# A hybrid decoder layer on one core: x and y loads queued behind weight loads, gamma and beta held in place, and the sum of probabilities on VectorE

## The chip, the core and the metric

The kernel runs on one core of a Trainium2 chip. The metric is device time in microseconds of one execution; the time before is the median of three runs. The engines are named as in the profile: PE is TensorE (PEld its weight loads), DVE is VectorE, ACT is ScalarE, POOL is GpSimd, and SP is SyncE, on whose queue every DMA of this kernel is issued. L122 is line 122 of the kernel before.

## The reference

One post-norm layer over a residual stream x of 1024 positions by 2048 channels, float32. Three mixers read the same x: attention with 8 heads of 128 and a forget gate, a short gated convolution, and causal pooling at four scales. Their gated outputs are concatenated, go through one output projection, and the result is normalised.

```python
proj = jnp.einsum('bsd,de->bse', x, w_in[l])
(q, k, v, g_att, fg, c_b, c_c, c_h, g_conv, p_u, g_pool) = jnp.split(proj, IN_SPLITS, axis=-1)
y_att  = forgetting_attention(q, k, v, fg, b_f[l]) * jax.nn.silu(g_att)     # heads apart
y_conv = short_conv_mixer(c_b, c_c, c_h, conv_w[l]) * jax.nn.silu(g_conv)
y_pool = multiscale_pool_mixer(p_u, pool_w[l], pool_scale[l]) * jax.nn.silu(g_pool)
y = jnp.concatenate([y_att, y_conv, y_pool], axis=-1)
y = jnp.einsum('bse,ed->bsd', y, w_out[l])
x = layer_norm(DEEPNORM_ALPHA * x + y, ln_g[l], ln_b[l])
```

Inside attention, per head: logits = q k / sqrt(128) + cum_q - cum_k, causal; p = softmax(logits); out = p v. The change touches the sum over the keys in this softmax, the loads of x for the last line, and the loads of ln_g and ln_b.

## The kernel before

**Numbers as pairs.** Every matmul operand is split into a high part, which ACT writes by a cast (L121), and a low part, which DVE writes by a subtraction (L122). A product is three matmuls (L128 high by high, L129 high by low, L130 low by high), all with 512 columns or fewer. So each weight tile `wh` of 128x512 costs one DMA load `wr` (256 KB), one ACT cast, one DVE subtraction, and feeds 12 matmuls. `t` is a tile of scores or probabilities, `pt` its split pair; `xy` and `xys` are split pairs of y or of sums of y blocks, loaded as `yr`.

**Stages.** The projection and the output product are each cut into 2x2 blocks and done with seven block products instead of eight. The first pass (0 to about 580 us) does four of the seven for 28 pairs of projection columns and keeps partial results in device memory. The second pass (to about 1256 us) does the other three for each pair; when a head's columns are ready, its attention runs beside the next pairs' matmuls, in small steps that `tick` takes from a list, one slot for every three matmul groups. Then come the output products, in the order y11, ys3, ys2, ys1, y22, y12, ys4, each twice (i = 0 and 1, the two halves of the columns), and the normalisation, whose steps for rows 512 and on run beside y12 and ys4, and for the first 512 rows beside and behind ys4.

**Attention of a head.** Scores are computed with the keys on the partitions, in blocks (n, j) of 128 keys j by up to 512 queries of half n: four blocks for n = 0, eight for n = 1. `find_top` takes the maximum over the keys through a small round trip by device memory (L746 writes `m_dram`, L748 loads it spread to all partitions as `mb`); `shift` (L759, DVE) subtracts it; `probs` (L765, ACT) takes the exponential; `parts` splits the block into `pt` (L121 on ACT, L122 on DVE); `values` multiplies by v on PE. `fold` (L712, and L710 for a first copy) adds a block to the running sum `m` over keys; before, it runs on POOL, just after the exponential. `invert` reduces that sum over the partitions (L735 to L745 on DVE) and makes the same round trip to `mb`, and `finish` multiplies by it (L798, DVE).

**What sets the order.** A scheduler with a simulated timeline places the instructions: each engine has one queue, worked off in order, and the scheduler may put an instruction ahead of others of the same queue if its simulated inputs and buffers are ready earlier. `keep_in_program_order` holds an instruction at its place; `issue_after` keeps the instructions of a block behind a given one on the same queue. Weight loads are made by `fill` (L184), in the order of `plan`; they take turns in four buffers `wr` with the `yr` and `wl` loads. `next_w` splits ahead: two weight tiles are held ready, from the ys2 product on four.

**Loads at the end.** `fetch` (L958) loads a y block, `load_x` (L1028) one of the 32 x tiles that are added to the result, into six buffers `st`, and `load_gb` (L1114) the four gamma and beta tiles of 512 KB, which are used first by the normalisation (L1144, L1145) beside y12.

Of the kernel before, what the change touches and what calls it, by code (L numbers as in the profile page):

```python
# [36 lines left out]
ALU = mybir.AluOpType  # L37
AX = mybir.AxisListType

P = 128  # L40
D = 2048
S = 1024
# [3 lines left out]
H = S // 2  # L46
# [27 lines left out]
def layer(ctx: ExitStack, tc: tile.TileContext, xt, x, wp, wf, b_f, conv_w, pool_w, pool_scale,  # L74
          w_out, ln_g, ln_b, out):
    nc = tc.nc
# [27 lines left out]
    def f4(name, tag):  # L104
        return tile_of([P, S], F32, name, tag)


    def hl(name, tag):
        return tile_of([P, 2, H], F32R, name, tag)

    def half(name, tag):
        return tile_of([P, H], F32, name, tag)
# [7 lines left out]
    def split(hi, lo, src):  # L120
        nc.scalar.copy(hi, src)  # L121
        nc.vector.tensor_tensor(lo, src, hi.bitcast(F32), ALU.subtract)  # L122

    def split_tile(t, src):
        split(t[:, 0], t[:, 1], src)
# [40 lines left out]
    def at(slot, step):  # L166

        while len(side) <= slot:
            side.append([])
        side[slot].append(step)  # L170
# [8 lines left out]
    stream = deque()  # L179
    ready = deque()  # L180
    plan = deque()
    ahead, n_split = [2], [0]

    def fill():  # L184
        while plan and len(stream) < 2:
            raw = half("wr", "wr")
            nc.sync.dma_start(raw, plan.popleft())
            stream.append(raw)

    def next_w():  # L190

        fill()
        while stream and len(ready) < ahead[0]:
            n_split[0] += 1
            t = hl("wh", "wx" if n_split[0] % 5 < ahead[0] - 2 else "wh")
            split_tile(t, stream.popleft())
            ready.append((t[:, 0], t[:, 1]))
            fill()
        return ready.popleft()
# [4 lines left out]
    def take(name, k, tag):  # L204
        xs[name, k] = hl("x" + name, tag)
        return xs[name, k]
# [460 lines left out]
    def attention(h, qs, ks, vt, gate):  # L667
        t, pt, v, o, top, down, total = {}, {}, {}, {}, {}, {}, {}
# [11 lines left out]
        def first(n, j):  # L680
            return max(0, j - 4 * n) * P
# [23 lines left out]
        def fold(kept, n, j, op, eng):  # L705
            c0 = first(n, j)
            if j == 1:
                kept[n] = half("m", "m")
                if c0:
                    eng.tensor_copy(kept[n][:, :c0], t[n, 0][:, :c0])  # L710
            prev = t[n, 0] if j == 1 else kept[n]
            eng.tensor_tensor(kept[n][:, c0:], prev[:, c0:], t[n, j][:, c0:], op)  # L712
# [49 lines left out]
        def probs(n, j):  # L762
            def go():
                tj, c0 = t[n, j], first(n, j)
                nc.scalar.activation(tj[:, c0:], tj[:, c0:], AF.Exp)  # L765
                if j:
                    fold(total, n, j, ALU.add, nc.gpsimd)
            return go

        def parts(n, j):  # L770
            def go():
                cw, th = min(first(n, j), 256), hl("pt", "pt")
                split(th[:, 0, cw:], th[:, 1, cw:], t[n, j][:, cw:])
                pt[n, j] = th
            return go

        def values(n, j):
# [26 lines left out]
        for n, s0, e0 in ((0, 3, 12), (1, 7, 20)):  # L804
            js = 4 * n + 4
            for j in range(js):
                at(s0 + j, scores(n, j))
                at(e0 + j, shift(n, j))
                at(e0 + j + 1, probs(n, j))
            for j in range(js):  # L810
                at(e0 + j + 2, parts(n, j))
                at(e0 + j + 3, values(n, j))
            at(s0 + js, find_top(n))
            at((4, 9)[n], turn_v(n))
            at(e0 + js + 2, invert(n))
            at(e0 + js + 7, finish(n))
# [141 lines left out]
    def fetch(name, k, slot):  # L958
        tag, src = BLOCKS[name]
        raw = []  # L960

        def load():
            raw.append(half("yr", "wr"))
            nc.sync.dma_start(raw[0], src(k))

        at(slot, load)
        at(slot + 2, lambda: split_tile(take(name, k, tag if isinstance(tag, str) else tag(k)), raw[0]))
# [60 lines left out]
    def load_x(name, i, st):  # L1028
        s, c = PLACE[name][0] + st, 2 * i + PLACE[name][1]
        xr = half("xr", "st")  # L1030
        nc.sync.dma_start(xr, x[s * P : s * P + P, c * H : c * H + H])
        return xr

    def residual_at(slot, i, st):

        env = {}

        def load():
            env["x"] = load_x("c22", i, st)

        def work():
            r = view("c22", i, st)
            nc.vector.scalar_tensor_tensor(r, env["x"], ALPHA, r, ALU.mult, ALU.add)
            stats_of(4 + st, r)

        at(slot, load)
        at(slot + 3, work)
# [4 lines left out]
    def preset_at(slot, name, i, st, tag):  # L1052


        env = {}

        def load():
            env["x"] = load_x(GOES_TO[name], i, st)

        def work():  # L1060
            acc = out_banks[name, i, st] = bank(tag)
            if name == "ys2":
                nc.scalar.copy(acc, view("c11", i, st))
            elif name == "ys4":
                nc.vector.scalar_tensor_tensor(acc, env["x"], ALPHA, view("c12", i, st), ALU.mult, ALU.add)
            else:
                nc.scalar.activation(acc, env["x"], AF.Copy, scale=ALPHA)

        if name != "ys2":
            at(slot, load)  # L1070
        at(slot + 3, work)
# [42 lines left out]
    def load_gb():  # L1114
        for src in (ln_g, ln_b):
            for hh in range(2):
                t = f4("gb", "gb")
                nc.sync.dma_start(t, src[hh * S : hh * S + S].partition_broadcast(P))
                gb.append(t)

    def norm_steps(s):
# [39 lines left out]
    def after(name, i):  # L1161
# [20 lines left out]
        if name == "y22":  # L1182
            for k in range(4 * i, 4 * i + 4):
                fetch("ys4", k, 1 + 2 * (k - 4 * i))
            if i == 0:
                at(9, load_gb)
            else:
                for st in range(4):
                    for n, step in enumerate(norm_steps(4 + st)):
                        at(1 + 5 * st + n, step)  # L1190
                for k in range(KH):
                    at(2 + 5 * k // 2, lambda k=k: load_last(1, k))
                    at(4 + 5 * k // 2, lambda k=k: split_last(1, k))
# [92 lines left out]
```

## Time and profile before

| | |
|---|---|
| time, median of 3 runs | 1631.89 us (1631.51 to 1632.08) |
| time of the profiled execution | 1629.22 us |
| its span, first to last instruction | 1627.5 us |
| mean granted clock of TensorE | 0.989 |
| POOL, folds of the sum (L712), 80 of them | 70.1 + 28.6 us |
| POOL, busy in all | 381.5 us |

The profiled execution lasts 1.7 us longer than its span, and 2.7 us less than the median of the runs. The rows of the views are read so: a group of instructions has line, engine, operation, tile written <- tiles read, shapes, count, then busy time, mean ns of one, and the engine's idle time before them with what ended it. A wait reads "engine tile line <- what ended it: us in total, times, longest". A window has its length, the busy time and count of PE, PEld, DVE, ACT and POOL, the granted clock, the mean busy share of the DMA engines, and GB/s. A timeline row has start, length (several instructions of one kind are merged), and in brackets the idle time before.

### The profile page before, as it was taken

Reading aid. Unit: us, or ns where it says so; the run is one execution under the profiler, and the core shown is the slowest. Engines: PE = TensorE matmul, PEld = TensorE weight load, DVE = VectorE, ACT = ScalarE, POOL = GpSimd, SP = SyncE. Lnnn points to the kernel's source line nnn. Section 1 sums busy time; section 2 is a strip of 40 time slices with the busy share of each in tenths; the row PEclk is TensorE's granted clock in tenths of the full one; section 3 lists DMA queues with packets and bytes.
Section 4 is the critical chain, followed back from the end, with each engine's and each line's share of the span. In section 5 each row is a group of like instructions: output and inputs, shape, how many; then the busy total and the mean of one; then the engine's idle time right before and its main releaser. Section 6 shows DMA issues by size and latency. Waiting matters only on the chain. (4 is left out here: it accounts for less than half of the span.)

```text
span 1627.5 us, 20130 instructions
## 1 busy us (share of the span) xinstructions
PE 1553.6 (95%) x6812; PEld 1254.3 (77%) x6812; DVE 1129.3 (69%) x1659; ACT 691.9 (43%) x1238; POOL 381.5 (23%) x303
## 2 busy tenths in 40 slices
PE   8999999999999999999999999999988998999986
PEld 6887888778787787788878777867766777788775
DVE  6754676666665656378787868577779875566797
ACT  4421221211121225566665656575666553444420
POOL 0232232222222220012232323343326322100000
PEclk9999999999999999999999999999999999999998
DMA  8756988887878667534545454535344445657572
GB/s 253 263 205 210 323 292 296 304 305 255 289 266 293 241 241 253 212 133 157 183 154 185 149 181 156 172 126 196 132 146 161 153 140 205 193 174 228 193 233 104
DMA packets 156807, 339.92 MB, mean 209 GB/s; under 512 B 17952, under 2 KB 27040, under 8 KB 156704
## 3 DMA queue, kind: packets, MB, share of 16 engines
q1 hardware_dynamic: 156704, 338.64, 61.2%
q8 instruction: 53, 0.87, 0.2%
q14 instruction: 50, 0.41, 0.1%
HBM read 247.28 MB, written 91.29 MB: 208 GB/s over the span
## 5 line engine op out<-in xcount | busy, mean ns | idle before, releaser
L122 DVE TENSOR_TENSOR wh<-wr,wh 128x512 fp32r<-128x512 f32 x264 | 199.4, 761 | 92.4 <-ACT wh L121 91.8
L121 ACT CAST wop<-wb 128x1024 fp32r<-128x1024 f32 x76 | 80.0, 1053 | 319.3 <-PE aux L129 139.2
L121 ACT CAST wh<-wr 128x512 fp32r<-128x512 f32 x264 | 161.5, 618 | 83.6 <-PE acc L130 27.9
L128 PE MATMUL acc<-x,wh 128*128 128x512 f32 x448 | 178.6, 399 | 3.3 <-ACT wh L121 3.3
L130 PE MATMUL acc<-x,wh 128*128 128x512 f32 x448 | 178.0, 397 | 3.4 <-DVE wh L122 3.4
L130 PE MATMUL aux<-xs,wop 128*128 128x512 f32 x448 | 175.5, 392 | 3.5 <-DVE wop L122 3.4
L129 PE MATMUL acc<-x,wh 128*128 128x512 f32 x448 | 176.3, 394 | 0.0
L128 PE MATMUL aux<-xs,wop 128*128 128x512 f32 x448 | 174.6, 390 | 0.0
L129 PE MATMUL aux<-xs,wop 128*128 128x512 f32 x448 | 174.4, 389 | 0.0
L122 DVE TENSOR_TENSOR wop<-wb,wop 128x1024 fp32r<-128x1024 f32 x76 | 102.7, 1352 | 27.1 <-ACT wop L121 27.0
L130 PEld LDWEIGHTS acc<-x,wh 128*128 128x128 f32 x448 | 84.7, 189 | 28.6 <-DVE wh L122 10.7
L130 PEld LDWEIGHTS aux<-xs,wop 128*128 128x128 f32 x448 | 84.1, 188 | 25.2 <-DVE wop L122 7.6
L128 PEld LDWEIGHTS acc<-x,wh 128*128 128x128 f32 x448 | 84.9, 190 | 22.5 <-ACT wh L121 7.2
L129 PEld LDWEIGHTS aux<-xs,wop 128*128 128x128 f32 x448 | 84.1, 188 | 17.7
L128 PEld LDWEIGHTS aux<-xs,wop 128*128 128x128 f32 x448 | 84.1, 188 | 17.5
L129 PEld LDWEIGHTS acc<-x,wh 128*128 128x128 f32 x448 | 85.0, 190 | 15.7
L130 PE MATMUL acc<-xs,wh 128*128 128x512 f32 x224 | 87.8, 392 | 3.4 <-DVE wh L122 3.4
L130 PE MATMUL acc<-xs,wop 128*128 128x512 f32 x224 | 88.0, 393 | 2.5 <-DVE wop L122 2.5
L122 DVE TENSOR_TENSOR pt<-t,pt 128x512 fp32r<-128x512 f32 (+1 forms) x96 | 84.5, 893 | 6.5 <-ACT pt L121 6.3
L128 PE MATMUL acc<-xs,wh 128*128 128x512 f32 x224 | 88.2, 394 | 0.0
L129 PE MATMUL acc<-xs,wh 128*128 128x512 f32 x224 | 87.4, 390 | 0.0
L128 PE MATMUL acc<-xs,wop 128*128 128x512 f32 x224 | 87.3, 390 | 0.0
(272 smaller groups left out, 3607.3 us busy)
## 6 DMA issues: line engine op xcount, KB each, us to landing
wb<-wp SPq DMA_DIRECT2D x116, 512.0 KB, 5.8
wr<-wp SPq DMA_DIRECT2D x112, 256.0 KB, 2.9
wo<-w_out SPq DMA_DIRECT2D x64, 256.0 KB, 6.0
o_dram<-wo SPq DMA_DIRECT2D x64, 256.0 KB, 4.5
wr<-o_dram SPq DMA_DIRECT2D x64, 256.0 KB, 2.8
t_dram<-wb SPq DMA_DIRECT2D x28, 512.0 KB, 5.8
a_dram<-ca SPq DMA_DIRECT2D x28, 512.0 KB, 3.8
b_dram<-cb SPq DMA_DIRECT2D x28, 512.0 KB, 4.6
```

Source lines behind the costliest of these rows:

```text
L121: nc.scalar.copy(hi, src)
L122: nc.vector.tensor_tensor(lo, src, hi.bitcast(F32), ALU.subtract)
L128: nc.tensor.matmul(acc, wh, xh, start=start, stop=False, **more)
L129: nc.tensor.matmul(acc, wh, xl, start=False, stop=False, **more)
L130: nc.tensor.matmul(acc, wl, xh, start=False, stop=stop, **more)
```

## The change

Three edits. `fill` remembers the last weight load that it traced, and the x loads and y loads are kept behind that one on the SP queue. The gamma and beta loads keep their place in the program. The fold of the sum moves from the step of the exponential to the step of the split, and from POOL to DVE.

```diff
     def fill():
         while plan and len(stream) < 2:
             raw = half("wr", "wr")
-            nc.sync.dma_start(raw, plan.popleft())
+            last_load[0] = nc.sync.dma_start(raw, plan.popleft()).ins
             stream.append(raw)
...
         def probs(n, j):
             def go():
                 tj, c0 = t[n, j], first(n, j)
                 nc.scalar.activation(tj[:, c0:], tj[:, c0:], AF.Exp)
-                if j:
-                    fold(total, n, j, ALU.add, nc.gpsimd)
             return go
 
         def parts(n, j):
             def go():
                 cw, th = min(first(n, j), 256), hl("pt", "pt")
                 split(th[:, 0, cw:], th[:, 1, cw:], t[n, j][:, cw:])
                 pt[n, j] = th
+                if j:
+                    fold(total, n, j, ALU.add, nc.vector)
             return go
...
         def load():
             raw.append(half("yr", "wr"))
-            nc.sync.dma_start(raw[0], src(k))
+            with tc.issue_after(last_load[0]):
+                nc.sync.dma_start(raw[0], src(k))
...
         xr = half("xr", "st")
-        nc.sync.dma_start(xr, x[s * P : s * P + P, c * H : c * H + H])
+        with tc.issue_after(last_load[0]):
+            nc.sync.dma_start(xr, x[s * P : s * P + P, c * H : c * H + H])
...
                 t = f4("gb", "gb")
-                nc.sync.dma_start(t, src[hh * S : hh * S + S].partition_broadcast(P))
+                tc.keep_in_program_order(nc.sync.dma_start(t, src[hh * S : hh * S + S].partition_broadcast(P)))
```

On VectorE, in the attention of a head (query half 1, blocks 0 to 3: `t` the probabilities, `pt` their split, `m` the sum, `wh` a weight split, L798 the end of the half before), the new order against the old:

```order
-L759 TENSOR_TENSOR t_5395<-t_5395,mb_5578 128x512
-L122 TENSOR_TENSOR pt_5728<-t_5353,pt_5728 128x512
-L122 TENSOR_TENSOR pt_5759<-t_5377,pt_5759 128x512
-L122 TENSOR_TENSOR wh_5738<-wr_5690,wh_5738 128x512
+L759 TENSOR_TENSOR t_5395<-t_5395,mb_5577 128x512
+L122 TENSOR_TENSOR pt_5726<-t_5353,pt_5726 128x512
+L712 TENSOR_TENSOR m_5759<-t_5353,t_5377 128x512
+L122 TENSOR_TENSOR pt_5756<-t_5377,pt_5756 128x512
+L712 TENSOR_TENSOR m_5759<-m_5759,t_5395 128x512
+L122 TENSOR_TENSOR wh_5736<-wr_5690,wh_5736 128x512
 L798 TENSOR_TENSOR pb_4809<-pb_4809,mb_5659 128x512
```

Two folds stand among the two splits; the fold of a block (here 5395) can stand ahead of that block's own split, since it needs the exponential alone.

On SP, at the end of ys3 and the start of ys2, before (`wr` weights from `o_dram`, `yr` sums of y, `xr` x tiles, `gb` gamma and beta):

```order
L964 DMA yr_11478<-sy_dram 128x512
L1031 DMA xr_12176<-x 128x512
L1031 DMA xr_12180<-x 128x512
L1031 DMA xr_12196<-x 128x512
L187 DMA wr_11486<-o_dram 128x512
L964 DMA yr_11500<-sy_dram 128x512
L1031 DMA xr_12198<-x 128x512
L1031 DMA xr_12217<-x 128x512
L1118 DMA gb_12711<-ln_g 128x1024
L187 DMA wr_11511<-o_dram 128x512
L1118 DMA gb_12713<-ln_g 128x1024
L964 DMA yr_11531<-sy_dram 128x512
```

With the change the weight and y loads stand there alone, and gamma and beta come about 105 DMAs later in the queue, among the first weight loads of y12 (`w_out`):

```order
L965 DMA yr_12670<-sy_dram 128x512
L187 DMA wr_12677<-w_out 128x512
L187 DMA wr_12696<-w_out 128x512
L1120 DMA gb_12711<-ln_g 128x1024
L1120 DMA gb_12713<-ln_g 128x1024
L1120 DMA gb_12715<-ln_b 128x1024
L1120 DMA gb_12717<-ln_b 128x1024
L187 DMA wr_12732<-w_out 128x512
L965 DMA yr_12746<-sy_dram 128x512
L187 DMA wr_12759<-w_out 128x512
L1033 DMA xr_12775<-x 128x512
```

The first x tile now stands where ys1 ends, and the others one to three at a time between weight loads.

On VectorE, at the end of the program (`bst` row statistics of the last product's two halves, 13300 and 13311; c_1909 and the three others the rows whose normalisation ends there), before:

```order
L1024 BN_STATS bst_12968<-acc_13300 128x6
L1133 TENSOR_SCALAR nt_13424<-mv_13420,nt_13424 128x1
L1024 BN_STATS bst_12968<-acc_13311 128x6
L1134 TENSOR_SCALAR nt_13424<-nt_13424,mv_13420 128x1
L1127 BN_AGGR mv_13490<-bst_12968 128x2
L1145 SCALAR_TENSOR_TENSOR c_1909_10844<-c_1909_10844,nt_13424,gb_12715 128x512
L1145 SCALAR_TENSOR_TENSOR c_2085_11772<-c_2085_11772,nt_13424,gb_12715 128x512
L1145 SCALAR_TENSOR_TENSOR c_1964_11125<-c_1964_11125,nt_13424,gb_12717 128x512
L1145 SCALAR_TENSOR_TENSOR c_2117_11953<-c_2117_11953,nt_13424,gb_12717 128x512
```

and with the change (L1147 is L1145 of before):

```order
L1025 BN_STATS bst_12968<-acc_13300 128x6
L1135 TENSOR_SCALAR nt_13424<-mv_13420,nt_13424 128x1
L1136 TENSOR_SCALAR nt_13424<-nt_13424,mv_13420 128x1
L1147 SCALAR_TENSOR_TENSOR c_1909_10844<-c_1909_10844,nt_13424,gb_12715 128x512
L1147 SCALAR_TENSOR_TENSOR c_2085_11772<-c_2085_11772,nt_13424,gb_12715 128x512
L1147 SCALAR_TENSOR_TENSOR c_1964_11125<-c_1964_11125,nt_13424,gb_12717 128x512
L1147 SCALAR_TENSOR_TENSOR c_2117_11953<-c_2117_11953,nt_13424,gb_12717 128x512
L1025 BN_STATS bst_12968<-acc_13311 128x6
L1129 BN_AGGR mv_13490<-bst_12968 128x2
```

Four L1145 moved from behind the last BN_STATS to ahead of it. On PE the change also puts the last two products in plain order: 96 matmuls of y12's second half, then 96 and 96 of ys4, where before 32 matmuls of ys4 stood among the last 20 of y12.

More of the change, by code (lines that the diff above doesn't have):

```diff
@@ L181, in layer @@
     plan = deque()
-    ahead, n_split = [2], [0]
+    ahead, n_split, last_load = [2], [0], [None]
     def fill():
```

## The prediction

> **What bounds the kernel now.** I read the page's busy times first, then the windows of the stretches that the change touches, then TensorE's waits in them, and last the timeline and the chain of waits at the places with the longest ones.
>
> ```profile
> span 1627.5 us, 20130 instructions
> PE 1553.6 (95%) x6812; PEld 1254.3 (77%) x6812; DVE 1129.3 (69%) x1659; ACT 691.9 (43%) x1238; POOL 381.5 (23%) x303
> ...
> 700.00:800.00 100.00, 100.00 (x466) 83.41 (x465) 77.30 (x130) 62.97 (x127) 23.64 (x24) 1.00 0.49 162
> ...
> 1200.00:1300.00 100.00, 88.05 (x389) 70.49 (x388) 85.48 (x140) 60.31 (x124) 39.00 (x34) 0.97 0.47 152
> 1300.00:1400.00 100.00, 89.47 (x382) 71.74 (x381) 61.08 (x100) 49.77 (x105) 19.88 (x20) 0.97 0.56 185
> 1400.00:1500.00 100.00, 100.00 (x443) 82.81 (x442) 62.49 (x97) 38.73 (x69) 6.26 (x4) 1.00 0.59 189
> ```
>
> TensorE (PE) is the bound: it is busy for 1553.6 of 1627.5 us, so everything that any change can win lies in the 73.9 us in which it is idle, and in the clock. Those idle times sit late. From 700 to 800 us, in the first heads of attention, there are none, from 1200 to 1400 us there are 22.5 us, and from 1400 to 1500 none again. (Columns: busy time of PE, PEld, DVE, ACT, POOL, then granted clock, DMA share, GB/s.) What ends them, from 560 to 1356 us (second pass and attention) and then to the end:
>
> ```profile
> PE aux L129 <- DVE pt L122: 12.7, 10, 2.5
> PE acc L128 <- ACT wh L121: 6.6, 4, 3.3
> ...
> PE acc L129 <- DVE wh L122: 4.9, 2, 4.1
> PE aux L128 <- ACT wh L121: 3.4, 2, 2.4
> PE acc L128 <- ACT wh L121: 1.7, 1, 1.7
> ```
>
> The largest is the low part of the split probabilities, `pt`, on VectorE (DVE): 12.7 us in ten waits. The last two rows are one place, 1378 to 1390 us (3.4 + 1.7 = 5.1 us in three waits). A long wait also costs clock:
>
> ```profile
> 1386.00:1394.00 8.00, 5.60 (x19) 4.16 (x18) 3.47 (x7) 5.95 (x12) 0.00 (x0) 0.79 0.70 226
> 1068.00:1078.00 10.00, 6.95 (x25) 5.07 (x24) 9.93 (x15) 4.36 (x11) 10.00 (x9) 0.85 0.23 71
> 1552.00:1562.00 10.00, 5.89 (x20) 4.65 (x20) 10.00 (x20) 2.36 (x4) 0.00 (x0) 0.83 0.76 247
> ```
>
> Behind the waits of 2.4, 2.5 and 4.1 us the granted clock is 0.79 over 8 us, 0.85 over 10 and 0.83 over 10: 8 x 0.21, 10 x 0.15 and 10 x 0.17 each give 1.5 to 1.7 us of lost clock. I price a dip at 1.6 us.
>
> [...]
>
> **Part 1: the sum of probabilities on VectorE.** Now GpSimd (POOL) folds, and VectorE splits and shifts beside it. One place out of eight alike, in the timeline, POOL first, then DVE, then PE:
>
> ```profile
> 912.88 1.63 POOL L871 TENSOR_TENSOR s3y<-pa 128x512 f32<-128x512 f32 x1
> 914.48 1.72 POOL L712 TENSOR_TENSOR m<-t,t 128x512 f32<-128x512 f32 x1
> 916.27 1.62 POOL L712 TENSOR_TENSOR m<-m,t 128x512 f32<-128x512 f32 x1
> ...
> 913.28 1.78 DVE L759 TENSOR_TENSOR t<-t,mb 128x512 f32<-128x512 f32 x1
> 914.99 3.45 DVE L122 TENSOR_TENSOR pt<-t,pt 128x512 fp32r<-128x512 f32 x2
> ...
> 916.80 0.50 PE L129 MATMUL aux<-pt,v 128*128 128x512 f32 x1 [1.29 <-DVE pt L122]
> ```
>
> The two splits take 1.72 us each, and end with the two folds, to a few hundredths; PE waits 1.29 us for the first. Free of POOL the same shape takes 0.68:
>
> ```profile
> L122 DVE TENSOR_TENSOR wlast<-wl,wlast 128x512 fp32r<-128x512 f32 x16 | 10.7, 682 | 1.1 <-ACT wlast L121 1.1
> ...
> 1066.46 0.42 DVE L759 TENSOR_TENSOR t<-t,mb 128x256 f32<-128x256 f32 x1
> 1066.80 0.28 DVE L723 TENSOR_TENSOR m<-m,t 128x128 f32<-128x128 f32 x1
> 1068.00 0.55 DVE L759 TENSOR_TENSOR t<-t,mb 128x384 f32<-128x384 f32 x1
> ...
> L122 DVE TENSOR_TENSOR pt<-t,pt 128x512 fp32r<-128x512 f32 x48 | 52.1, 1098 | 6.1 <-ACT pt L121 6.1
> L759 DVE TENSOR_TENSOR t<-t,mb 128x512 f32<-128x512 f32 x48 | 46.5, 982 | 15.1 <-DMA mb<-m_dram 15.1
> L122 DVE TENSOR_TENSOR pt<-t,pt 128x256 fp32r<-128x256 f32 x32 | 18.3, 573 | 0.3 <-ACT pt L121 0.3
> L122 DVE TENSOR_TENSOR pt<-t,pt 128x384 fp32r<-128x384 f32 x16 | 14.7, 918 | 0.1
> ...
> L712 POOL TENSOR_TENSOR m<-m,t 128x256 f32<-128x256 f32 (+1 forms) x64 | 70.1, 1095 | 59.8 <-ACT t L765 57.7
> L712 POOL TENSOR_TENSOR m<-t,t 128x384 f32<-128x384 f32 (+1 forms) x16 | 28.6, 1786 | 39.4 <-ACT t L765 34.5 <-DVE pa L908 4.9
> ```
>
> Removed from POOL: 80 folds (70.1 + 28.6 us) and eight small copies. Added to DVE, per head: query half 0 needs a copy of 128 columns and folds of 384, 256 and 128; half 1 four folds of 512 and one each of 384, 256, 128. That is 0.21 (estimate, below the 0.28 of two inputs) + 1.25 + 4 x 0.68 + 1.25 = 5.4 us, 43 us over eight heads. Given back: `pt` takes 48 x 1.098 + 32 x 0.573 + 16 x 0.918 = 85.7 us and would take 48 x 0.682 + 32 x 0.42 + 16 x 0.55 = 55.0 free of POOL, 31 too much; the 48 full shifts 48 x (0.982 - 0.682) = 14 too much. The ends for the relief are nothing (if the other POOL work takes the folds' place) and 31 + 14 = 45, and somewhat more with `wh` and the narrow shifts. POOL's folds start with the same exponential that releases the split, so I take it near the upper end: 40 us, an estimate. **VectorE's load then stays about as it is** (+3 us), but the part on PE's path, the split, comes first or nearly so.
>
> What PE wins: at the place above the shift (1.78) is held up by L871, which stays, and the split goes from 1.75 to 0.68, so of 1.29 us some 1.1 goes. Three heads look like this. I give the change two thirds of the 12.7 us, 8.4, and take 2.4 off, because in about half of the places the order puts a fold of 0.6 us ahead of the next split or weight split (the rows in the section on the change). One dip goes with the 2.5 us wait. Term: **-6.0 - 1.6 = -7.6 us**. Its bounds are +8 (the second rival) and -12.7 - 3.2. Behind a fold on DVE wait the weight splits `wh`; PE holds two of them ready, so 0.6 us is covered except where a `mb` transfer has just emptied the queue. POOL's remaining work stands off the path; the invert, which waited for POOL at L735, now waits for a fold just before it, and I cost that at nothing.
>
> **Part 2: x and gamma, beta leave the place at 1370 us.** The chain of waits there, then ACT's timeline, then the landing times of `gb`:
>
> ```profile
> 1371.63 6.60 DMA xr<-x
> 1378.30 6.58 DMA yr<-sy_dram
> ...
> 1389.84 2.71 DMA wr<-o_dram
> ...
> 1379.02 0.62 ACT L121 CAST wh<-wr 128x512 fp32r<-128x512 f32 x1 [2.15 <-DMA wr<-o_dram]
> 1383.06 0.62 ACT L121 CAST wh<-wr 128x512 fp32r<-128x512 f32 x1 [2.85 <-DMA wr<-o_dram]
> 1388.46 2.28 ACT L121 CAST wh<-wr 128x512 fp32r<-128x512 f32 x4
> ...
> DMA to landing us min/median/max: 6.0/7.0/7.9
> ```
>
> Six x tiles (256 KB each) and four gamma and beta tiles (512 KB each), 3.6 MB, are issued among the weight and y loads, long before anybody wants them. A load takes 6.6 us there instead of 2.7, ACT stands idle for it, and PE waits three times. In the new order of SP none of the ten is left there. The loads' own chain (2.7 + cast + split) stays, so I take 4.0 of the 5.1 us and the dip: **-4.0 - 1.6 = -5.6 us**; bounds 0 and -6.7.
>
> The ten transfers are not gone. The x tiles now come one or two at a time between weight loads; bursts of x tiles between 1400 and 1500 us cost PE nothing before either (its row above is 100 of 100). Gamma and beta move to just behind the fifth weight load of y12, some 145 us later, and the sixth load, a y load and the next weight load queue behind their 2 MB for 6 to 8 us. PE has four split weights ready there, about 11 us. I cost it at 0, with 4 us (6.6 - 2.7) as the upper end, plus a dip.
>
> **Part 3: the end.** The last normalisations fill VectorE (10.00 of 10 us in the window from 1552, above), and PE has its longest wait (4.1 us) for a weight split behind them.
>
> ```profile
> 1614.30 0.70 DVE L1024 BATCH_NORM_STATS2 bst<-acc 128x6 f32<-128x512 f32 x1 [0.22 <-PE acc L130]
> ...
> 1615.22 2.67 DVE L1145 SCALAR_TENSOR_TENSOR c<-c,nt,gb 128x512 f32<-128x512 f32 x4
> ...
> 1621.12 2.74 DVE L1145 SCALAR_TENSOR_TENSOR c<-c,nt,gb 128x512 f32<-128x512 f32 x4
> ```
>
> After the last matmul VectorE now does two groups of four L1145, 2.67 and 2.74 us. In the changed order the first group stands ahead of the last BN_STATS, beside PE's last 24 matmuls: **-2.6 us**. The long wait itself stays: between the eleventh and the twelfth weight split of y12 the old order has 14 other full-width instructions on VectorE and the new one 16, at 0.67 us each (2.67 / 4) 9.4 and 10.7 us. I cost that at 0, bounds -4 and +4.
>
> Sum: -7.6 - 5.6 - 2.6 = -15.8. I round to -15, as removed waits seldom vanish whole. The profiled execution took 1629.22 us, 2.67 below the median of the runs (1631.89); 1629.2 - 15 = 1614.2, and in the runs' terms **1616.9 us**.
>
> **The rivals.** (a) The waits pass on: PE is freed from `pt`, then waits for `wh` or `mb` a little later, and only a third of part 1 (-2.5) and the end (-2.6) are left with half of part 2 (-2.8): 1624. For it: waits for ACT's `wh` are 6.6 us of PE's idle time before 1356 us, and part 1 doesn't touch them. (b) Gamma and beta hit y12: the loads behind them are 4 us late, VectorE's unbroken stretch starts later, and 4 + 1.6 us come back: 1622.5. (c) **Slower:** the folds are blocked where POOL still works. POOL is busy for 39 of the 100 us from 1200; the folds are 98.7 / 8 = 12 us a head, so some 25 us of means, differences and sums of y stay there. If the 40 us of relief are cut by half, VectorE carries 20 us more, most of it in the four heads after 1000 us that already have waits; with 16 us of it on PE's path and parts 2 and 3 kept (-8.2) that is 1640. It decides once the folds' mean passes about 0.8 us. Against it: from 700 to 800 us DVE is idle for 23 of 100 us, and nothing of POOL but some 10 us stays. (d) The change not doing what it says is out: the rows of the orders show all three moves.
>
> [...]
>
> **How the numbers follow.** Forecast 0.55, (a) 0.2, (b) 0.13, (c) 0.08, and 0.04 for a larger gain. The range, 1608 to 1632: below, part 1 at -10 with two dips (-3.2), part 2 whole (-6.7) and the end (-2.6) make -22.5 and 1609; above, it takes in (a) and (b) and what both together would leave (1630), and it leaves (c) out. A measurement of this kernel can tell about 0.2%, 3.3 us, from no change: faster is below 1628.6, slower above 1635.2. Faster 0.8, same 0.11, slower 0.09.
>
> **What would show it.** Right: `pt` 128x512 near 0.75 us on average, DVE's busy time within 10 us of 1129; PE's wait for `pt` below 5 us; no wait over 1 us from 1370 to 1392; one L1145 group behind the last matmul. Wrong: L712 on DVE over 0.8 us; PE's waits for `wh` up by what those for `pt` fall; a new wait near 1520 to 1535 us behind `gb`; the long wait at 1552 us grown.

## The result and the profile after

| | before | after |
|---|---|---|
| time, median of four runs each | 1631.99 us (1631.51 to 1632.19) | 1622.75 us (1622.35 to 1624.12) |
| ratio, 95% interval | | 0.994 (0.9926 to 0.9953) |
| time of the profiled execution, its span | 1629.22, 1627.5 us | 1624.12, 1622.3 us |

The change is 9.2 us faster; the forecast was 15, its range held the time. Measured again (x1 below), the ratio was 0.991 (0.9887 to 0.9932), 14.7 us. The page of the change, then PE's waits from 560 to 1356 us, VectorE's groups in attention, and windows (columns as before):

```profile
span 1622.3 us, 20045 instructions
PE 1548.7 (95%) x6812; PEld 1253.5 (77%) x6812; DVE 1127.6 (70%) x1747; ACT 690.8 (43%) x1238; POOL 285.0 (18%) x215
```
```profile
PE acc L128 <- ACT wh L121: 7.9, 9, 1.2
PE acc L130 <- DVE wh L122: 7.2, 8, 2.8
PE aux L128 <- ACT pt L121: 6.7, 4, 2.3
PE aux L128 <- DVE m L725: 5.1, 3, 3.3
PE aux L129 <- DVE pt L122: 3.5, 7, 1.9
...
PE acc L129 <- DVE wh L122: 1.6, 1, 1.6
```
```profile
L122 DVE TENSOR_TENSOR pt<-t,pt 128x512 fp32r<-128x512 f32 x48 | 33.4, 698 | 1.7 <-ACT pt L121 1.7
L712 DVE TENSOR_TENSOR m<-m,t 128x512 f32<-128x512 f32 x24 | 16.3, 681 | 0.0
```
```profile
1200.00:1300.00 100.00, 89.33 (x388) 71.39 (x387) 86.86 (x158) 62.04 (x128) 27.88 (x24) 0.95 0.49 156
1300.00:1400.00 100.00, 96.80 (x432) 78.74 (x431) 62.91 (x118) 52.80 (x111) 9.46 (x9) 1.00 0.52 164
1400.00:1500.00 100.00, 98.77 (x436) 81.48 (x435) 65.24 (x102) 38.52 (x69) 6.27 (x4) 1.00 0.59 187
```

VectorE's load stayed (1129.3 to 1127.6), the split of a full block went from 1098 to 698 ns, and PE's wait for `pt` from 12.7 to 3.5 us. But its wait for ScalarE's half of `pt` grew to 6.7 us, from this row of before:

```profile
PE aux L128 <- ACT pt L121: 2.1, 2, 1.8
```

From 1200 to 1300 us hardly anything was won and the clock is lower (0.95, before 0.97); from 1300 to 1400 PE has 96.8 busy us instead of 89.5; from 1400 on there is a wait that was not there. Then the end, VectorE's timeline, with one group of L1147 (L1145 before) behind the last statistics, as forecast:

```profile
1607.98 2.74 DVE L1147 SCALAR_TENSOR_TENSOR c<-c,nt,gb 128x512 f32<-128x512 f32 x4
1611.39 0.70 DVE L1025 BATCH_NORM_STATS2 bst<-acc 128x6 f32<-128x512 f32 x1 [0.68 <-PE acc L130]
...
1615.88 2.74 DVE L1147 SCALAR_TENSOR_TENSOR c<-c,nt,gb 128x512 f32<-128x512 f32 x4
```

**Where the time went.** I counted PE's matmuls with weight tiles in order and compared the start of the same one in two traces. The table gives, for each run, by how many us a stretch is longer (+) or shorter than in the first profile of before (stretches in its time); the last column is the span's difference. The experiments' rows stand here too, since all are read from this table. Below, "the tail" is the stretch from 1476 us to the last matmul, and "the end" is what lies behind it.

| run | 0 to 703 | 703 to 1350 | 1350 to 1412 | 1412 to 1476 | 1476 to last matmul | behind it | span |
|---|---|---|---|---|---|---|---|
| before again (x9) | +3.4 | -1.3 | -0.2 | 0.0 | +2.5 | 0.0 | +4.4 |
| the change | +8.4 | -6.8 | -9.6 | 0.0 | +5.1 | -2.3 | -5.2 |
| the change again (x1) | +2.8 | -4.0 | -9.6 | 0.0 | +6.6 | -2.3 | -6.5 |
| sum alone (x2) | -0.8 | -4.2 | -6.4 | 0.0 | +3.1 | 0.0 | -8.3 |
| loads alone (x3) | +1.7 | -1.3 | -7.9 | 0.0 | +4.8 | -2.3 | -5.1 |
| gamma, beta free (x4) | +2.3 | -5.1 | -5.3 | 0.0 | +1.5 | 0.0 | -6.5 |
| sum on POOL, behind the split (x5) | +2.1 | -3.2 | -7.2 | 0.0 | +5.5 | -2.3 | -5.1 |
| sum on DVE, ahead of the split (x6) | +1.0 | -1.8 | -9.6 | 0.0 | +5.8 | -2.3 | -6.9 |
| x free (x7) | +0.1 | -5.8 | -8.6 | +0.7 | +5.9 | -2.3 | -10.0 |
| gamma, beta in ys1 (x8) | +3.7 | -3.0 | -10.3 | +3.9 | +1.8 | 0.0 | -4.0 |
| copies held (x10) | +4.7 | -22.6 | -7.2 | +0.3 | +6.1 | -2.3 | -21.1 |
| normalisation held (x11) | +1.1 | -9.5 | -10.5 | 0.0 | +1.6 | +2.1 | -15.1 |
| copies held, sum on POOL (x12) | +6.5 | -13.0 | -8.5 | +1.3 | +6.6 | -2.3 | -9.5 |

### The profile page after: what moved, and what is told of

It reads as the page before. It is cut to its first block, busy times and chain, and to the rows that moved or that the text cites. A ratio compares the mean times of both kernels' runs of the same rounds, so it can differ in the third digit from the quotient of the medians.

```text
span 1622.3 us, 20045 instructions
## 1 busy us (share of the span) xinstructions
PE 1548.7 (95%) x6812; PEld 1253.5 (77%) x6812; DVE 1127.6 (70%) x1747; ACT 690.8 (43%) x1238; POOL 285.0 (18%) x215
## 5 line engine op out<-in xcount | busy, mean ns | idle before, releaser
L128 PEld LDWEIGHTS acc<-x,wh 128*128 128x128 f32 x448 | 85.0, 190 | 26.5 <-ACT wh L121 10.9
L130 PE MATMUL acc<-xs,wop 128*128 128x512 f32 x224 | 87.9, 393 | 2.6 <-DVE wop L122 2.6
L128 PE MATMUL acc<-xs,wop 128*128 128x512 f32 x224 | 87.2, 389 | 0.0
L129 PE MATMUL acc<-xs,wop 128*128 128x512 f32 x224 | 87.2, 389 | 0.0
```

The costliest lines, as they stand in the source:

```text
L128: nc.tensor.matmul(acc, wh, xh, start=start, stop=False, **more)
L129: nc.tensor.matmul(acc, wh, xl, start=False, stop=False, **more)
L130: nc.tensor.matmul(acc, wl, xh, start=False, stop=stop, **more)
```

## The experiments

Each ratio is against runs of before on the same chip, made together with those of the run. Single executions of one program differ by several us (25 of before in the batch of x5 to x8: 1623.32 to 1641.42 us). The stretches differ less, but the seven profiles that have the same sum and the same copies (the change, x1, x2, x4, x7, x8, x11) still lie between -3.0 and -9.5 from 703 to 1350 us, so a difference of 2 or 3 us between two single profiles shows nothing in that stretch.

**x1, the change again.**

> The changed kernel once more, for its size and for how far two executions of one program lie apart. If the first pass (the same program in both kernels) differs only by chance, its end lies some microseconds away from that of the first profile of the change (which was 7.5 us later than in the profile of before), and the stretches behind it keep their differences. If the change itself slows the first pass, the five waits of 1.4 to 1.9 us in it come again at the same places. Time: 0.994 of before.

Ratio 0.991 (0.9887 to 0.9932). The first pass, the same instructions in both kernels, ends 6.4 us late in the first profile of the change and 2.3 late here; in the other runs it ends between 0.6 early and 5.6 late, and in before itself, run again, 3.6 late (x9). The first column is chance, then, and it hid most of what the first profile had won: without it the change wins 13.6 and 9.3 us in its two profiles.

**x2 and x3, one part at a time.** x2 has the fold's move alone, x3 everything but that.

```diff
 x2:  in parts:  +    fold(total, n, j, ALU.add, nc.vector)      loads as before
 x3:  in probs:  +    fold(total, n, j, ALU.add, nc.gpsimd)      loads as in the change
```

> The sum of probabilities on VectorE, loads as before. Theory (the three parts add up): -6 to -7.6 us, 1625, with the waits of 1378 to 1390 us and the long wait at 1552 us as before. Rival (the waits pass on to ScalarE's and VectorE's weight splits): -2.5 us or less, 1629.5. In both: pt 128x512 near 0.70 us.

> Loads of x, y, gamma and beta as in the change, the sum of probabilities on GpSimd as before. Theory (parts add up): the burst's place gives -9.7 us, the end -2.3, and the tail gives back 3 to 5 for a hole between the weight splits of y12: about -7 to -9, 1624. Rival (the burst's place gains so much only because the waits ahead of it had gone with the sum): -5 at that place, -2 to -4 in all, 1629.

Ratios 0.9937 (0.9915 to 0.9959) and 0.994 (0.9918 to 0.9961), about 10 us each, against 14.7 for both in the same batch: the parts seem not to add up, though the intervals of the three are wide (some 3.5 us each way). From 703 to 1350 us the sum gives its few us and the loads nothing that can be told from before run again (-1.3 both). The place from 1350 to 1412 us is where they overlap: both edits shorten it, the sum alone by 6.4, the loads alone by 7.9, together 9.6. Here are PE's waits in it, of before, of the sum alone, and of the loads alone:

```profile
PE aux L128 <- ACT wh L121: 3.4, 2, 2.4
PE acc L128 <- ACT c L1077: 1.9, 1, 1.9
PE acc L128 <- ACT wh L121: 1.7, 1, 1.7
```
```profile
PE aux L128 <- ACT wh L121: 3.3, 2, 2.4
PE acc L128 <- ACT wh L121: 0.6, 1, 0.6
```
```profile
PE aux L128 <- ACT wh L121: 1.3, 1, 1.3
PE acc L128 <- ACT c L1079: 0.5, 1, 0.5
```

The middle row of before is a wait at 1355 us for ScalarE to evacuate a bank, which the prediction had not counted. ScalarE's timeline of before there, with PE's matmul that waits:

```profile
1355.95 0.62 ACT L121 CAST xys<-yr 128x512 fp32r<-128x512 f32 x1 [1.63 <-DMA yr<-sy_dram]
1356.47 2.04 ACT L1077 COPY c<-acc 128x512 f32<-128x512 f32 x4
```
```profile
1357.10 0.50 PE L128 MATMUL acc<-wh,xys 128*128 128x512 f32 x1 [1.95 <-ACT c L1077]
```

The four evacuations stand in ScalarE's queue behind a cast that waits for a y tile. Why the tile is there in time with the sum alone was not tried; that either edit removes or shortens the wait is shown. The waits explain only some 3 of the 6.4 us of the sum alone (7.0 us of them in before, 3.9 here). The rest is the clock: over these 62 us it is 0.94 in before (62 x 0.06 = 3.7 us), with two dips (0.79 over the 8 us from 1356, and over the 8 us from 1386), and 1.00 with the sum alone, although the wait of 2.4 us that has a dip behind it in before still stands there. The last section has more on dips that fail to come.

**x4, gamma and beta free.**

```diff
-  tc.keep_in_program_order(nc.sync.dma_start(t, src[...].partition_broadcast(P)))
+  nc.sync.dma_start(t, src[...].partition_broadcast(P))
```

> The change with gamma and beta not held in place: their four loads stand at about 1370 us again, as in before, x and y loads behind the weight loads. If the 2 MB of gamma and beta make the stall at 1370 us: the three waits come back there (+3 to +6), and the tail loses its hole (-3 to -5) if the hole is the burst's: near 1622. If the hole is VectorE's order (15 instructions between two weight splits in the change, 11 here), the waits at 1540 to 1555 us shrink but do not go: 1624 to 1626. If the x tiles made the stall at 1370 us, no wait comes back there: 1618.

Ratio 0.9924 (0.9904 to 0.9944). The stall comes back as one wait, and the loads of gamma and beta make it (the x tiles are elsewhere here):

```profile
1375.61 1.93 PE L128 MATMUL acc<-wh,xys 128*128 128x512 f32 x4 [4.16 <-ACT wh L121]
```

In exchange the tail costs 1.5 instead of 5 to 7 us, and the end gives its 2.3 back. The three come to about 2 us for the hold (4.3 + 2.3 - 4.4), by the ratios 2.3, and neither is clear of the noise: **holding gamma and beta moves a loss; that it removes any of it is not shown.**

**x5 and x6, engine and place of the fold.** x5 keeps it on POOL and moves it behind the split; x6 has it on VectorE and ahead of the split.

```diff
 x5:  in parts:  +    fold(total, n, j, ALU.add, nc.gpsimd)
 x6:  in probs:  +    fold(total, n, j, ALU.add, nc.vector)
```

> The change, but the fold of the sum of probabilities stays on GpSimd and only its place moves, behind the split. Theory (the engine counts: VectorE and GpSimd hold each other up): pt 128x512 stays above 0.95 us, PE's waits for pt come back (about 12 us from 560 to 1356), the time is that of the loads alone, about 4 us above the change. Rival (the place counts: a fold that starts later no longer meets the split): pt near 0.75 us and the time of the change within 2 us.

> The change, but VectorE's fold is written right behind the exponential, ahead of the split. Theory (VectorE is on PE's path in the late heads): folds of 0.68 us stand ahead of splits, PE's waits for pt grow from 3.5 to 6 to 8 us, the time is 3 to 5 us above the change. Rival (VectorE has slack, or the order comes out nearly the same): within 2 us of the change.

Ratios 0.9969 (0.9948 to 0.9989) and 0.9966 (0.9941 to 0.9992). VectorE's group of full splits, of x5 and of x6:

```profile
L122 DVE TENSOR_TENSOR pt<-t,pt 128x512 fp32r<-128x512 f32 x48 | 52.2, 1099 | 6.1 <-ACT pt L121 6.1
```
```profile
L122 DVE TENSOR_TENSOR pt<-t,pt 128x512 fp32r<-128x512 f32 x48 | 35.4, 739 | 2.2 <-ACT pt L121 2.2
```

With the fold on POOL the split stays at 1099 ns, with the fold on VectorE it is fast in both places (698 and 739): the engine counts. But x5 doesn't test the rival, that a fold which starts later would no longer meet the split. POOL's instructions come in the same order in x5 as in before, and the first fold still starts half a microsecond ahead of the first of the two splits:

```profile
916.27 1.72 POOL L712 TENSOR_TENSOR m<-t,t 128x512 f32<-128x512 f32 x1
```
```profile
916.78 3.46 DVE L122 TENSOR_TENSOR pt<-t,pt 128x512 fp32r<-128x512 f32 x2
```

No run delayed a fold on POOL. In x6 the stretch from 703 to 1350 us wins only 1.8, against 5.5 on average in the seven profiles named above. PE's waits for VectorE's half of `pt` stay low (3.8 us); those for ScalarE's half rise to 10.9. So the expectation had about the right price for this stretch, but the wrong engine; how the earlier folds delay ScalarE's half was not followed up.

**x7, x free; x8, gamma and beta in ys1.** ("The run before this one" in the next text is x4.)

```diff
 x7:  load_x:    -    with tc.issue_after(last_load[0]):
 x8:  after(ys2, 1):  +    at(3 + 4 * m, lambda m=m: load_gb(m))      m = 0 to 3, one tile each, held
      after(y22, 0):  -    at(9, load_gb)
```

> The change, but with the x loads free again, so that six x tiles stand near 1370 us; y loads, gamma and beta as in the change. With gamma and beta free instead (the run before this one) a wait of 4.2 us stood at 1371 us, where the change has one of 0 to 1.2. If the x tiles stall the weight loads as well: 3 to 5 us of waits from 1350 to 1410, and 3 to 5 us above the change. If gamma and beta alone make the stall: no wait above 1.3 us there, and the time within 2 us of the change.

> The change with gamma and beta loaded one at a time in the first pass of ys1 (about 1425 to 1455 us), where PE has no waits, and not in y12. Theory (gamma and beta in y12 delay the weight loads there): the stretch from 1408 us to the last matmul, 5 to 6.6 us longer than in before with the change, comes to about 1.5 us longer (as with gamma and beta free), while the end behind the last matmul is 2.3 us longer again (VectorE's order with three L1145 groups last): 2 to 3 us below the change, with the place at 1370 us as quiet as in the change. Rival (the tail is held by the order of VectorE or by the pace of its own loads): the waits of 2 to 5 us at 1540 to 1550 us stay, and the time is within 1.5 us of the change or above it.

Ratios 0.9921 (0.9894 to 0.9949) and 0.9937 (0.9913 to 0.9961). x7: the place at 1370 us loses only 1.0 of its 9.6, and the time is that of the change: the x loads cost little there, the hold of x does little. x8: both halves of the theory held in the table (the tail at +1.8, the end at 0), though waits of the size that the rival named are still there (2.2 us at 1542, 2.6 at 1552). But the loads made a new wait of 2.0 us at 1455 us, with a granted clock of 0.79 over the 8 us behind it (1.7 us), and so 3.9 us were lost where PE had never waited. None of the three places tried is free for these 2 MB.

**x9, before again.**

> The kernel before once more, for its trace: every difference so far is taken against one profile of it. If that profile was typical, this one has the same waits of 1 us and more from 700 us on, within some tenths: 1.3 us for pt at 830, 916 and 1003, 2.5 at 1072, 2.2 at 1183, three waits for the evacuations (1.0, 1.9, 1.9) at 1300, 1326 and 1355, three at 1378 to 1390, and 4.1 at 1552; the first 560 us may differ by some microseconds.

1633.65 us. From 703 to 1476 us the two profiles of before agree within 1.5 us, with the same waits (1.3, 1.3, 1.3, 2.5, 2.2 for `pt`, 1.0, 1.9, 2.1 for evacuations, 4.1 at 1556). These two profiles differ by up to 3.4 us in a stretch; the seven of the change and its variants spread wider (6.5 us from 703 to 1350).

**x10, ScalarE's copies held.** One of the waits for ScalarE that replaced those for VectorE has a cause that the trace shows. ScalarE's timeline of before, then of the change (x1), at the same place, then PE's matmul of the change there:

```profile
1107.76 0.85 ACT L738 COPY quads<-part 32x16 f32<-32x16 f32 x4 [1.65 <-DVE part L736]
1108.63 0.51 ACT L121 CAST pt<-t 128x384 fp32r<-128x384 f32 x1
1109.42 0.59 ACT L528 COPY acc<-pb 128x512 f32<-128x512 f32 x1 [0.28 <-DMA pb<-b_dram]
1109.95 0.40 ACT L121 CAST pt<-t 128x256 fp32r<-128x256 f32 x1
```
```profile
1110.37 0.59 ACT L528 COPY acc<-pb 128x512 f32<-128x512 f32 x1 [5.62 <-DMA pb<-b_dram]
1110.90 0.84 ACT L738 COPY quads<-part 32x16 f32<-32x16 f32 x4
1111.76 0.71 ACT L121 CAST pt<-t 128x256 fp32r<-128x256 f32 x2
```
```profile
1112.22 0.39 PE L128 MATMUL aux<-pt,v 128*128 128x256 f32 x1 [1.85 <-ACT pt L121]
```

L528 copies a stored partial sum into a bank. In the new order one of these stands ahead of the casts of `pt`, and ScalarE stands for 5.6 us until its tile has landed. At the other three of PE's four waits for ScalarE's `pt` in x1 no copy that waits stands ahead of the cast. The one of 1.75 us at 1167 is in before too (1.75 at 1163). At the one of 0.92 at 1202 and at the longest, below, ScalarE works off an ACT_TABLE_LOAD (an instruction of 1.28 us that writes no tile) and activations just ahead of the cast:

```profile
1264.69 0.50 PE L128 MATMUL aux<-pt,v 128*128 128x512 f32 x1 [2.45 <-ACT pt L121]
```

```diff
-        nc.scalar.copy(acc, block)
+        tc.keep_in_program_order(nc.scalar.copy(acc, block))
```

> The change, with ScalarE's copies of stored sums into banks (L528) held in the order in which the code is written, so that the one that waits 5.5 us for a DMA near 1105 us no longer stands ahead of the casts of pt. Theory (the waits for ScalarE's pt in heads 5 to 8 are such copies): the wait of 1.8 to 2.2 us near 1110 and the lost clock behind it go, -3 us from 1052 to 1350, if PE doesn't wait for the later copies themselves. Rival (the waits only follow from the later start of the shifts, or pass on once more): 1052 to 1350 stays within 1.5 us of the change.

Ratio **0.9808 (0.9783 to 0.9832)**, 1602.2 us: by far the best of all, and far more than expected. (Its profiled execution, 1608.2 us, is the slowest of its five.) ScalarE's waits in L528 for `pa` and `pb` from 640 to 1345 us, in before, in the change (x1) and here:

```profile
ACT acc L528 <- DMA pa<-a_dram: 15.0, 8, 3.8
...
ACT acc L528 <- DMA pb<-b_dram: 7.0, 4, 3.1
```
```profile
ACT acc L528 <- DMA pa<-a_dram: 17.1, 8, 5.2
...
ACT acc L528 <- DMA pb<-b_dram: 10.6, 3, 5.6
```
```profile
ACT acc L528 <- DMA pb<-b_dram: 2.6, 1, 2.6
...
ACT acc L528 <- DMA pa<-a_dram: 1.2, 1, 1.2
```

22.0 us before, 27.7 in the change, 3.8 here. PE waits 0.9 us for ScalarE's `pt` (7.0 in x1) and 1.9 for VectorE's, and from 703 to 1350 us the run is 18.6 us ahead of x1. That is not all the copies' waiting. PE's idle time from 703 to 1350 us of each run falls by 10.4 us (31.9 to 21.5), of which its waits for `pt` are some 7.5; the rest of the 18.6 lies in time that the profile counts as busy, with a granted clock of 0.98 in x1 and 0.99 here. The theory had looked for 3 us from 1052 us on, but almost half of the 18.6 comes before that, where no wait for ScalarE's `pt` had stood. The hold also moves other instructions, on PE and SP too, and how much of the gain is the copies' own stays open.

**x11, normalisation held.**

```diff
-  nc.vector.scalar_tensor_tensor(r, src, mv[:, 0:1], g, ALU.subtract, ALU.mult)
+  keep(nc.vector.scalar_tensor_tensor(r, src, mv[:, 0:1], g, ALU.subtract, ALU.mult))     and the second one
```

> The change, with the normalisation pieces of the four lower row groups held in the order in which the code is written. Then no more than 8 instructions stand between two of VectorE's weight splits in y12 (15 in the change, 11 in before). Theory (the hole at 1540 to 1555 us is VectorE's order, bunched by the late gamma and beta): both waits of 2 to 5.6 us there fall below 1.5 us, -4 to -7 us from 1498 to the last matmul; the end grows by 2.3 since three L1147 groups stand last again: 2 to 5 us below the change. Rival (VectorE's load or the pace of the loads holds the tail): the waits come elsewhere between 1500 and 1600, and the time is that of the change or 2 us above it.

Ratio 0.9914 (0.989 to 0.9937), no better than the change; the tail shows why. PE's waits from 1500 to 1600 us, of the change (x1) and of x11:

```profile
PE acc L129 <- DVE wh L122: 7.8, 2, 5.6
```
```profile
PE acc L128 <- ACT wh L121: 2.1, 1, 2.1
PE acc L129 <- DVE wh L122: 0.9, 2, 0.7
PE aux L129 <- DVE wh L122: 0.4, 2, 0.2
```

The two long waits are gone with gamma and beta still loaded in y12. That they are VectorE's queue and not late weight loads, the trace of x1 shows at the longer one: ScalarE has the weight tile cast some 6 us before VectorE, busy without a break (20 of the 20 us from 1530) with normalisations, sums and statistics, comes to split it.

```profile
1543.80 0.62 ACT L121 CAST wh<-wr 128x512 fp32r<-128x512 f32 x1 [0.35 <-DMA wr<-w_out]
```
```profile
1550.51 0.67 DVE L122 TENSOR_TENSOR wh<-wr,wh 128x512 fp32r<-128x512 f32 x1
```
```profile
1551.23 0.80 PE L129 MATMUL acc<-wh,xy 128*128 128x512 f32 x1 [5.56 <-DVE wh L122]
```

The tail is 5.0 us shorter than in x1, and 4.4 of it are lost again behind the last matmul, where three groups of the last step of the normalisation (four instructions each) stand in place of one. So x11 takes work out of the tail as well as spreading it, and doesn't tell the order of VectorE's work from its amount.

**x12, copies held and the sum on POOL.**

```diff
 x10 with, in probs:  +    fold(total, n, j, ALU.add, nc.gpsimd)      and none in parts
```

> The copies L528 held as in the run before (which came to 0.981 of before, 1602.2 us, with 3.8 us of ScalarE standing in L528 for a DMA where the change has 27.7), and the sum of probabilities back on GpSimd behind the exponential; loads as in the change. Theory (the sum's own gain was hidden because PE, freed from pt, met ScalarE's blocked copies; without them it is what the prediction gave it, 7.6 us): the waits for pt of 1.3 to 2.5 us are back, and it is 7 to 9 us above that run, ratio about 0.986. Rival 1 (the sum is worth what it measured with the copies as they were, 2 to 4 us): ratio 0.983. Rival 2 (held copies alone do it all, the waits for pt are hidden as well): ratio 0.981, waits for pt under 4 us.

Ratio 0.9923 (0.9909 to 0.9937), against 0.9808 with the sum on VectorE. From 703 to 1350 us x10 is 9.6 us ahead of x12 (-22.6 and -13.0); by the ratios it is 19 us, but the two were not timed together. PE's waits for VectorE's `pt` came back to 5.5 us, less than expected; the loss is the 7 to 9 us of the first theory or more. The other comparison is with x3, which has the sum on POOL and the copies free: the stretch says that the hold alone gives 11.7 us there (-13.0 and -1.3), the ratios about 3 us, not clear of the noise (0.9923 and 0.994). So the large gain of x10 is seen in the time only with the two edits together. The copies were not held together with x11's normalisation.

## Why the prediction was right, and where not

1. **The sum, -7.6: right in direction, too large.** Split time, the time of a full fold (681 ns, so no blocked folds and no rival (c)), VectorE's load and the wait for `pt` came out as written. (One reading was off: the two splits at 915 us end 0.55 us after the two folds, not with them. The narrow folds took more than assumed, 639 ns for 256 columns where 420 were put in.) The seven profiles with the fold on VectorE behind the split and the copies as they were win 5.5 us on average from 703 to 1350 us, the four with it on POOL (x3, x5 and both of before) 1.4: the term measures -4.0. What failed is the step "two thirds of the 12.7 us, less 2.4 for folds": the wait fell by 9.2, but 4.6 of it came back as the wait for ScalarE's half (2.1 to 6.7), and some 3 as waits for weight splits (ScalarE's 6.6 to 7.9, the new row of 1.6). The dip of 1.6 us that was to go with it was not seen to go: the clock from 703 to 1350 us is 0.99 in before and 0.98 in x1. Rival (a) had the mechanism, and named `wh`: at 831, 917 and 1004 us a wait of 1.3 us for `pt` stands in before, and at the same places of x1 one of 1.05 us for ScalarE's `wh`. In the later heads it is ScalarE's half of `pt`, once behind a copy that waits 5.6 us for a DMA. With the copies held the sum measures 9.6 (x10 against x12, one profile each), as forecast or more; which of the instructions moved by the hold had hidden it is not shown.
2. **The burst at 1370 us, -5.6: too small.** It measures -9.6 with both parts, -7.9 and -7.2 with the loads alone (x3, x5), beyond the bound of -6.7; one wait of 1.2 us was left there in the first profile. The sum had left out the wait at 1355 us (1.95 us) and the clock behind it (0.79 over 8 us). Free again, gamma and beta bring 4.3 us back (x4), the x tiles 1.0 (x7).
3. **Gamma and beta in y12, 0: wrong.** The eight profiles with them there and the normalisation free lose 5.8 us on average in the tail, the five with them early 1.8: +4.0, within the upper end (5.6). Rival (b) had the price. Its reason, late weight loads, is not what the longest wait shows (x11): VectorE's work stands between two weight splits. And some 1.6 of the 4.0 us fall at 1478 us, at a wait of 1.2 to 1.9 us in the change's two profiles, over 30 us before these loads are issued (1511 to 1515 us); what makes that one was not tried. The long wait of 4.1 us, costed at 0 with the orders' 14 and 16 instructions, became two of 2.9 and 2.8 in one profile and 2.3 and 5.6 in the other.
4. **The end, -2.6: right.** It measures -2.3 in every run with that order.
5. **The sum of terms, -15.8.** Averaged over the change's two profiles: -5.4, -9.6, +5.9 and -2.3 make -11.4, between the 9.2 and the 14.7 us that the two timings gave. Two terms that were 3.6 and 4.0 us too good (the sum, gamma and beta) were half paid by a wait that had not been counted (4.0). That the time lay as near to the forecast as it did is in part luck: errors of opposite sign.

## What to carry to other kernels

When a wait is taken from one of two engines that prepare an operand together, read what stands at the head of the other's queue: here half of the wait that was removed (4.6 of 9.2 us) came back as a wait for the other engine, and on top of the change, holding one kind of its instructions in written order was worth more than the change itself (ratio 0.981 with both, 0.991 with the change alone). A transfer that is moved can take its loss along, as these 2 MB did at three places (4.3, 4.0 and 3.9 us); look first at what its consumers do to the queue at the new place. And price a stretch from several profiles, since a stretch that no edit had touched differed by up to 7 us between runs.

## What the runs showed of the hardware

In these runs a clock dip behind a stall was not certain. In the change a wait of 1.78 us at 1115 us was followed by a granted clock of 0.79 over 8 us; with the sum alone the same wait at 1107 us (1.78), and one of 2.4 at 1377, were followed by full clock (1.00 over 8 us each). Windows of the change, then of x2:

```profile
1117.00:1125.00 8.00, 7.84 (x30) 6.43 (x31) 6.35 (x13) 4.70 (x10) 0.11 (x1) 0.79 0.35 109
```
```profile
1108.00:1116.00 8.00, 7.35 (x35) 6.24 (x36) 6.32 (x14) 5.17 (x11) 0.11 (x1) 1.00 0.30 91
1377.00:1385.00 8.00, 5.74 (x25) 4.77 (x26) 3.88 (x6) 5.16 (x11) 0.00 (x0) 1.00 0.71 238
```

The prediction counted each removed stall of over 2 us with 1.6 us of clock; by these rows it is a chance, not a price, and the dip of the change came behind 1.78 us of waiting. What decides which stall is followed by one, no run shows.
